# A hybrid attention and recurrence block on one core: attention in steps of one segment, and another split of the filler

## The chip, the cores and the metric

The kernel runs on one core of one Trainium2 chip. The core has five engines: PE (TensorE, matrix products), DVE (VectorE), ACT (ScalarE), POOL (GpSimd) and SP (SyncE, which here only issues DMAs). The time is the device time of one execution in microseconds, the lower the better; 4504.49 us is the median of 3 runs (4469.48 to 4522.03).

## What is computed

The input x is 4096 x 1024 in float32; 16 learned rows stand ahead of it, so T = 4112. After an RMS norm, one matrix product with w_in gives the inputs of two branches. The reference, cut to what matters:

```python
u = rmsnorm(h, norm_w)
p = u @ w_in                                  # 1024 columns to q, k, v, forget logits, gates, r, k, v, ...
# attention, 8 heads of 64, block of 128 queries, causal
s = q @ k.T / 8 + c[q] - c[k]                 # c: running sum of log sigmoid(forget logits)
o = softmax(where(k_pos <= q_pos, s, -1e30)) @ v * silu(z)
# recurrence, 8 heads, S is 64 x 64, one step per row
S = S * w_t + (S @ a_t) b_t + v_t k_t;  y = S @ r_t        # then group norm, bonus, silu gate
out = rmsnorm(h + concat(o, y) @ w_out, final_norm_w)[16:]
```

## The kernel before, in words

The kernel is one program; the order of instructions on every engine is made when it is built, by a planner that walks all instructions by priority (`tc.high_priority(offset=...)`, offsets in PR, L37: the larger the offset, the earlier) and places each when its inputs are ready in a model of the time. The `Ordered` wrapper (L54) around VectorE, ScalarE and TensorE adds ordering by hand: in mode "note" it remembers the last instruction, in mode "behind" it ties each new one after the remembered one.

Stages. (1) Weights are scaled and split into two float16 parts, x is normalised, split and transposed (to L384). (2) The recurrence (`rwkv_chain`, L818) in 33 sub-blocks of up to 128 rows, each of 4 chunks of 32 rows, each chunk in 3 hops: 387 hops. Beside every hop run the preparation of later sub-blocks (`beside`, L911) and filler: the generator `projections` (L636) makes the matrix products with w_in in four passes over 17 blocks of 256 rows. Pass 0 is the recurrence's own input (`in_proj`, L410), pass 1 q, k, v, z of heads 4 and 5 (`qk_block` L463, `vz_block` L480), pass 2 those of heads 0 to 3, pass 3 those of heads 6, 7 and the recurrence's gate (`gate_block`, L533). One unit of filler is 48 matmuls of 256 columns; a full block of passes 1, 2, 3 has 2, 4, 4 units. A hop is credited with RATE = 0.33 units (L941). (3) Attention. `head_load` (L986) fetches K, V and the column term cb of one 1024-key chunk of a head, `fetch` (L1108) calls it ahead of need, `projected` (L981) runs filler until the rows that are needed have been projected.

`attention(h, i, ...)` (L1014) is a generator for one block of 128 queries, W = 16 + 128 (i + 1) keys, in segments of SEG = 1024 keys (one to five). First part: for all segments scores on PE into ps_q (two buffers), and DVE's L1051 adds cb, writes sp and keeps the running maximum mt; L1057 makes nm. Second part, for all segments: ACT exponentiates sp in place (L1065), copies it to the high float16 part hl (L1071), POOL (60%) or DVE subtracts for the low part (L1076), and SP transposes hl into ht by DMA (L1078). Third part: the output matmuls ps_o, two for each 128 keys (L1086 to L1093), then row scale and gate (L1096 to L1101). Buffers: NSP = 9 of sp, NHL = 6 of hl and of ht. `advance` (L1191) runs the first part of block i, then the third part of block i - 1, then the second part of block i.

Between blocks of the first seven heads the loop at L1205 takes filler from `late` (the rest of `projections`, then `rwkv_out`, L1146, which multiplies the recurrence's half with w_out: 32 blocks of 128 rows, 24 matmuls of 512 columns each, counted 0.5 each) in proportion to the work done; `projected` takes from it without counting. In the last head (L1247), `out_prep` (L1225) and `out_rows` (L1236) do the attention's half of the output product, the sum, the last norm and the store, at the lowest priority.

Matmuls recorded at L67 were made while a mode of `Ordered` was set (in the recurrence), those at L92 without.

Of the kernel before, what the change touches and what calls it, by code (L numbers as in the profile page):

```python
# [40 lines left out]
NHL, NSP = 6, 9  # L41
# [6 lines left out]
RATE = 0.33  # L48
LEAD = 6
PARTS = ((0, 0), (0, 1), (1, 0))  # L50
# [26 lines left out]
def hymba_kernel(ctx: ExitStack, tc, x, meta, norm_w, w_in, b_f, mu_shift, w0, w_up, a0, a_up,  # L77
# [884 lines left out]
    with ExitStack() as fs:  # L962
# [18 lines left out]
        def projected(p, t):  # L981

            while done[PASS_OF[p]] * NB < min(t, SEQ + 1):
                next(late)
# [26 lines left out]
        nseg = 0  # L1011
        qz = {}

        def attention(h, i, head, dst):  # L1014

            nonlocal nseg
            p, hp = divmod(h, 2)
            q0 = 64 * hp
            if i % 4 == 0:
                g = min(4, NT - i)  # L1020
                t0 = N_META + i * P
                projected(p, t0 + g * P)
                Q = at.tile([P, 2, 4 * P], F16, tag="Q", name="Q")
                for a in range(2):
                    DQ.dma_start(Q[64 * a:64 * a + 64, :, :g * P],
                                 qk_d[p][a:a + 2, q0:q0 + 64, t0:t0 + g * P].rearrange("v p t -> p v t"))
                Zt = at.tile([P, 4, HD], F32, tag="Z", name="Zt")
                DQ.dma_start(Zt[:, :g], zf_d[p][t0:t0 + g * P, q0:q0 + 64].rearrange("(s t) e -> t s e", t=P))
                qz[h] = (Q, Zt)
            Q, Zt = qz[h]  # L1030
            W = N_META + P * (i + 1)
            qs = slice((i % 4) * P, (i % 4) * P + P)
            sps = []
            mt = at.tile([P, 8], F32, tag="mt", name="mt", bufs=4)
            ni = 0
            for a0 in range(0, W, SEG):
                sp = at.tile([P, SEG], F32, tag="sp", name="sp", bufs=NSP)
                sps.append(sp)
                for a in range(a0, min(a0 + SEG, W), 1024):
                    b = min(a + 1024, W)  # L1040
                    c, o = chunk(a)
                    o = a - o
                    ps = ps_q.tile([P, 1024], F32, tag="q", name="ps_q")
                    for a2 in range(a, b, 512):
                        b2 = min(a2 + 512, b)
                        dg = max(a2, min(b2, W - P))
                        for v in range(2):
                            mm(ps[:, a2 - a:b2 - a], Q[:, v, qs], head[c][0][:, a2 - o:b2 - o], v == 0, v == 1 and dg == b2)
# [237 lines left out]
```

## Time and profile before

| | us |
|---|---|
| median of 3 runs | 4504.49 |
| lowest, highest | 4469.48, 4522.03 |
| the profiled execution | 4462.28 |
| its span, first to last instruction | 4460.4 |
| PE busy | 3912.1 (88%) |
| DVE, ACT, POOL busy | 2956.9, 2122.7, 2230.5 |

Everything that follows is read from the one profiled execution. A busy time is the time in which an engine has a matmul or another operation in work; the ends of matmuls are modelled, so a run of short matmuls counts a little more than it takes. "PEclk" or "clock" is the granted share of TensorE's full clock. "DMA" is the mean busy share of the core's 16 DMA engines, where packets of different queues that overlap on one engine count twice, so that it can be over 1. In a line of waits stand the waiting operation, what ended the wait, the total in us, the number of waits and the longest.

### The profile page before, as it was taken

The page shows a single profiled execution, that of the slowest core. Times are in us where ns is not written, and L with a number is a line of the kernel's source. Part 1 is how long each engine was busy: PE and PEld are TensorE (multiplying, and loading weights), DVE is VectorE, ACT ScalarE, POOL GpSimd, SP SyncE. Part 2 cuts the span into 40 slices and gives each one's busy share as a digit, 9 for nine tenths or more (in the row PEclk, how much of TensorE's full clock was granted, in tenths as well). Part 3 has the DMA queues.
Part 4 walks back from the last instruction along what each step waited for, and adds up shares of the span by engine and source line. Part 5 has one row for each costly group of instructions (what it writes and reads, how often), then busy time and mean ns, then how long its engine had stood idle before and what let it go on. Part 6 is the DMA issues. An engine that isn't in the chain of part 4 may idle for free. (4 is left out here: it accounts for less than half of the span.)

```text
span 4460.4 us, 106426 instructions
## 1 busy us (share of the span) xinstructions
PE 3912.1 (88%) x42336; PEld 3012.8 (68%) x42336; DVE 2956.9 (66%) x6217; ACT 2122.7 (48%) x4338; POOL 2230.5 (50%) x3289
## 2 busy tenths in 40 slices
PE   5689999999989899998878878888888878978888
PEld 4577777777767677777656655666666656666566
DVE  5346665666667666752878978677787758646774
ACT  5433333333333233321666757577676747524552
POOL 4137565667666665762445545444454435332340
PEclk8899999999876899899999989999999989989989
DMA  9963223323222344324999999999999999999995
GB/s 265 262 172 93 79 79 97 87 75 90 74 70 79 85 138 121 98 88 141 196 213 229 216 193 227 199 216 227 208 212 234 212 203 223 258 270 242 198 218 185
DMA packets 1702644, 755.37 MB, mean 169 GB/s; under 512 B 1444601, under 2 KB 1639601, under 8 KB 1692162
## 3 DMA queue, kind: packets, MB, share of 16 engines
q1 hardware_dynamic: 1489346, 502.84, 55.8%
q10 hardware_dynamic: 194624, 170.08, 15.3%
q0 software_dynamic: 18176, 75.66, 5.6%
q8 instruction: 332, 5.44, 0.5%
q14 instruction: 166, 1.36, 0.1%
HBM read 278.97 MB, written 158.50 MB: 98 GB/s over the span
## 5 line engine op out<-in xcount | busy, mean ns | idle before, releaser
L1076 POOL TENSOR_TENSOR hl<-sp,hl 128x1024 f16<-128x1024 f32 (+7 forms) x384 | 719.7, 1881 | 517.3 <-ACT hl L1071 440.7
L1065 ACT ACTIVATE sp<-sp,nm 128x1024 f32<-128x1024 f32 (+8 forms) x672 | 644.5, 962 | 223.5 <-DVE nm L1057 175.6
L1071 ACT ACTIVATE hl<-sp 128x1024 f16<-128x1024 f32 (+8 forms) x672 | 568.2, 872 | 366.1 <-DMA ht<-hl 239.4
L92 PE MATMUL ps_o<-Vt,ht 128*128 128x64 f16 (+3 forms) x8960 | 559.5, 211 | 180.6 <-DMA ht<-hl 177.8
L92 PE MATMUL ps_q<-K,Q 128*128 128x512 f16 (+4 forms) x2432 | 596.9, 366 | 119.4 <-DVE mt L1051 118.3
L758 POOL TENSOR_TENSOR tm<-X,Am 128x248 f32<-128x248 f32 (+30 forms) x1023 | 498.1, 487 | 376.6 <-DMA Am<-a_d 290.1
L92 PEld LDWEIGHTS <-ht 128*128 128x128 f16 (+1 forms) x8960 | 466.9, 100 | 315.0 <-DMA ht<-hl 204.9
L92 PEld LDWEIGHTS <-wu 128*128 128x128 f16 (+1 forms) x5476 | 513.1, 102 | 194.8 <-ACT wu L160 28.1
L760 POOL TENSOR_TENSOR X<-X,tm 128x248 f32<-128x248 f32 (+30 forms) x1023 | 517.7, 506 | 76.6
L67 PEld LDWEIGHTS <-wu 128*128 128x128 f16 (+1 forms) x4988 | 454.5, 101 | 114.3 <-issue 26.0
L1051 DVE CUSTOM_DVE_ANT_0 sp<-ps_q,cb,mt 128x1024 f32<-128x1024 f32 (+8 forms) x416 | 436.1, 1048 | 80.3 <-PE ps_q L92 40.8
L1076 DVE TENSOR_TENSOR hl<-sp,hl 128x1024 f16<-128x1024 f32 (+8 forms) x288 | 383.2, 1333 | 99.3 <-ACT hl L1071 98.1
L92 PEld LDWEIGHTS <-Q 128*128 128x128 f16 x2432 | 221.8, 100 | 294.8 <-issue 150.2
L67 PE MATMUL ps_in<-fu,wu 128*128 128x256 f16 x3108 | 416.0, 285 | 3.4 <-DVE car L67 3.4
L1051 DVE CUSTOM_DVE_ANT_0 sp<-ps_q,cb,scs 128x1024 f32<-128x1024 f32 (+7 forms) x256 | 297.6, 1164 | 71.2 <-POOL hl L1076 43.9
L92 PE MATMUL ps_qk<-fu,wu 128*128 128x256 f16 x1632 | 237.7, 280 | 24.0 <-DVE t1k L500 18.5
L92 PE MATMUL ps_vz<-wu,fu 128*128 128x256 f16 x1644 | 247.6, 284 | 1.0 <-ACT th L544 0.6
L92 PE MATMUL ps_p<-OH,yH 128*128 128x512 f32 x512 | 221.5, 433 | 29.0 <-DVE oxt L1144 27.5
L1070 POOL MEMSET hl<- 128x224 f16 x256 | 72.4, 287 | 336.8 <-DMA ht<-hl 318.4
L92 PE MATMUL ps_zr<-fu,wu 128*128 128x256 f16 x1536 | 224.8, 285 | 8.0 <-DVE nm L1057 6.3
L67 PE MATMUL psz<-UV,SC 32*64 32x64 f32 (+1 forms) x4128 | 222.4, 232 | 3.0 <-ACT UV L67 2.2
L92 PE MATMUL ps_p<-OH,yL 128*128 128x512 f32 x512 | 209.6, 411 | 0.0
(350 smaller groups left out, 6976.6 us busy)
## 6 DMA issues: line engine op xcount, KB each, us to landing
fu<-u_d POOLq DMA_DIRECT2D x32, 1024.0 KB, 6.8
fu<-u_d SPq DMA_DIRECT2D x30, 1024.0 KB
pr<-p_d SPq DMA_DIRECT2D x32, 832.0 KB
p_d<-prt SPq DMA_DIRECT2D x96, 256.0 KB
u_d<-u SPq DMA_DIRECT2D x16, 1024.0 KB
Am<-a_d SPq DMA_DIRECT2D x128, 128.0 KB
Q<-qk_d ACTq DMA_DIRECT2D x128, 128.0 KB
oxt<-in_x_dram ACTq DMA_DIRECT2D x32, 512.0 KB
```

The source lines that it names most:

```text
L67: r = f(*args, **kw)
L92: PE.matmul(o, lhsT=l, rhs=r, start=start, stop=stop)
L758: G.tensor_tensor(out=tm[:, :, :k], in0=bc(X[:, :, s:s + 1], [P, 8, k]), in1=bc(Am[:, s * C + s + 1:s * C + C].unsqueeze(1), [P, 8, k]), o ...
L760: G.tensor_tensor(out=X[:, :, s + 1:], in0=X[:, :, s + 1:], in1=tm[:, :, :k], op=ALU.add)
L1051: V.tensor_tensor_reduce(out=sp[:, a - a0:b - a0], in0=ps[:, :b - a], in1=head[c][2][:, a - o:b - o], scale=scs[:, p, 0, hp:hp + 1], scala ...
L1065: A.activation(sp[:, :n], sp[:, :n], AF.Exp, bias=nm[:, 0:1], accum_out=nm[:, 1 + a // SEG:2 + a // SEG])
L1070: G.memset(hl3[:, :, n:], 0.0)
L1071: A.activation(hl3[:, 0, :n], sp[:, :n], AF.Copy)
L1076: eng.tensor_tensor(out=hl3[:, 1, :n], in0=sp[:, :n], in1=hl3[:, 0, :n], op=ALU.subtract)
```

## The change

`attention`, `finish` and `advance` go. In their place `pipeline()` makes one step for each segment: the scores of segment sg of the next block (`scores`, PE in mode "note"), then the weights of segment sg of this block (`weights`: exponential, copy, subtract, transpose), then the output products of the segment that was put aside LAG = 6 steps earlier (`output`, whose first matmul is tied behind the last scores matmul made). The arithmetic of the three is as before. Buffers: hl 5 (was 6), sp 7 (was 9), ht 9 (was 6), nm 12 (was 8), Zt 3 (was 2), o1 2 (was 4). Q and Zt of the next four blocks are loaded two blocks ahead. Filler: RATE falls to 0.265, four units (AHEAD) are taken before the first step, a step takes its share at once rather than a block, `projected` counts what it takes, a block of `rwkv_out` counts 1.0. The last head's output rows follow the blocks whose outputs have been made. Cut to its core (`scores`, `weights` and `output` hold the statements of `attention` and are shortened):

```diff
-NHL, NSP = 6, 9
+NHL, NSP, NHT = 5, 7, 9
-RATE = 0.33
+AHEAD = 4
+RATE = 0.265
+LAG = 6
         def projected(p, t):
+            nonlocal spent
             while done[PASS_OF[p]] * NB < min(t, SEQ + 1):
-                next(late)
+                spent += next(late)
+        def load_q(n):
+            if n >= len(steps) or n in qz:
+                return
...
+            Zt = at.tile([P, 4, HD], F32, tag="Z", name="Zt", bufs=3)
...
+        def scores(n, sg):
...
+            if sg == 0:
+                fetch(hx, i)
+                load_q(n - n % 4)
+                if n % 4 == 2:
+                    load_q(n + 2)
...
+        def weights(n, sg):
...
+            ht = at.tile([P, 2 * SEG // P, P], F16, tag="ht", name="ht", bufs=NHT)[:, :2 * nt]
+            hl = at.tile([P, 2 * SEG], F16, tag="hl", name="hl", bufs=NHL)[:, :2 * nt * P]
...
+            SP.dma_start_transpose(out=ht, in_=hl)
+        def output(n, sg):
...
+            PE.mode = "behind"
+            for j in range(nt):
...
+                mm(pso, ht[:k, j], Vj[:k], jt == 0, False)
+                PE.mode = None
+                mm(pso[:, 0:HD], ht[:k, nt + j], Vj[:k, 0:HD], False, jt * P + k == W)
...
                 for _ in rwkv_out(op, OW):
-                    yield 0.5
+                    yield 1.0
-        left = sum(max(0, NFULL - done[i]) * n for i, n in ((1, 2), (2, 4), (3, 4))) + 0.5 * NT
+        left = sum(max(0, NFULL - done[i]) * n for i, n in ((1, 2), (2, 4), (3, 4))) + NT
+        pend = []
+        def pipeline():
+            for n in range(-1, len(steps)):
+                ka = segs(n) if n >= 0 else 0
+                kb = segs(n + 1) if n + 1 < len(steps) else 0
+                for sg in range(max(ka, kb)):
+                    if sg < kb:
+                        PE.mode = "note"
+                        scores(n + 1, sg)
+                        PE.mode = None
+                    if sg < ka:
+                        weights(n, sg)
+                        pend.append((n, sg))
+                    while len(pend) > LAG or pend and pend[0][0] < n - 4 or (n == len(steps) - 1 and sg == ka - 1 and pend):
+                        output(*pend.pop(0))
+                    if sg < ka:
+                        yield n, min(SEG, width_of(steps[n][1]) - sg * SEG) + 2 * P // ka
+        allwork = 7 * sum(width_of(i) + 2 * P for i in range(NT))
+        with tc.high_priority(offset=PR[5]):
+            while spent < AHEAD:
+                spent += next(late)
+        while now < 7 * NT:
+            with tc.high_priority(offset=PR[3]):
+                now, cols = next(att)
+            work += cols
+            with tc.high_priority(offset=PR[5]):
+                while spent * allwork < work * left:
...
+        while True:
+            with tc.high_priority(offset=PR[4]):
+                if next(att, None) is None:
+                    break
+            output_rows((pend[0][0] if pend else len(steps)) - 7 * NT)
+        output_rows(NT)
+        out_rows(NT - 1, *ready)
```

## Rows read from the trace of the kernel before

**Rows 1.** Stages: us; PE, PEld, DVE, ACT, POOL busy (count); clock, DMA share, GB/s

```profile
400.00:1983.00 1583.00, 1524.65 (x19788) 1197.39 (x19785) 1022.48 (x2241) 519.32 (x1299) 1033.36 (x2026) 0.91 0.32 89
1983.00:2083.00 100.00, 99.92 (x915) 89.20 (x914) 28.43 (x76) 17.05 (x42) 30.41 (x43) 1.00 0.30 111
...
2126.00:3610.00 1484.00, 1251.79 (x13128) 931.26 (x13125) 1160.41 (x2446) 1010.22 (x1949) 716.72 (x673) 0.93 1.14 215
...
3740.00:4061.00 321.00, 275.77 (x1826) 201.66 (x1825) 188.32 (x357) 140.30 (x248) 118.98 (x95) 0.92 1.17 262
4061.00:4361.00 300.00, 249.08 (x1882) 181.74 (x1881) 210.41 (x379) 163.68 (x289) 104.22 (x81) 0.91 1.05 214
4361.00:4460.00 99.00, 86.43 (x392) 68.20 (x390) 49.75 (x74) 24.62 (x44) 8.11 (x15) 0.97 0.50 184
```

**Rows 2.** PE in order of time, at the recurrence's end: start, us, what

```profile
1982.55 0.66 PE L67 MATMUL psd<-ident,Y 128*128 128x128 f32 x4
1983.28 5.41 PE L67 MATMUL ps_vz<-wu,fu 128*128 128x256 f16 x48
1988.53 5.40 PE L67 MATMUL ps_qk<-fu,wu 128*128 128x256 f16 x48
```

**Rows 3.** ACT in order of time, from there to the first softmax block

```profile
2083.41 1.18 ACT L891 ACTIVATE Yt<-psd,gbT,gwT 128x32 f32<-128x32 f32 x4
...
2084.62 8.52 ACTq L995 DMA_DIRECT2D K<-qk_d  x10
...
2123.92 0.41 ACT L1065 ACTIVATE sp<-sp,nm 128x144 f32<-128x144 f32 x1 [0.39 <-DVE nm L1057]
```

**Rows 4.** Output matmuls ps_o alone, by stretches of one head: us, PE, DVE, ACT busy

```profile
2350.00:2588.00 238.00, 70.22 (x1120) 6.83 (x32) 6.65 (x32) 0.94 1.15 218
...
3615.00:3940.00 325.00, 69.82 (x1072) 6.46 (x32) 6.46 (x32) 0.91 1.14 228
3940.00:4361.00 421.00, 80.53 (x1311) 7.01 (x34) 7.01 (x34) 0.92 1.08 232
```

**Rows 5.** DMA queues, 2126 to 3610 us (q1 SP, q10 ACT, q0 POOL): packets, MB, share

```profile
q1 hardware_dynamic: 857200, 215.47, 84.1%
q10 hardware_dynamic: 91392, 48.60, 16.4%
q0 software_dynamic: 12624, 53.23, 12.5%
```

**Rows 6.** Waits from 2126 to 3610 us: total, times, longest

```profile
ACT hl L1071 <- DMA ht<-hl: 173.2, 92, 15.9
...
PE ps_o L92 <- DMA ht<-hl: 113.8, 59, 11.0
...
PE ps_q L92 <- DVE mt L1051: 96.0, 85, 7.1
...
DVE sp L1051 <- POOL hl L1076: 45.5, 20, 15.7
```

**Rows 7.** Waits of SP's queue in the same stretch

```profile
SPq L1078 <- PE ps_o L92: 170.5, 84, 7.7
```

**Rows 8.** Matmuls ps_p alone after the attention

```profile
4361.00:4460.00 99.00, 79.75 (x336) 62.10 (x336) 19.05 (x29) 0.97 0.50 184
```

**Rows 9.** Filler matmuls by shape, PE, 2126 to 3610 us: busy, mean ns, idle before

```profile
L92 PE MATMUL ps_vz<-wu,fu 128*128 128x256 f16 x1443 | 221.0, 285 | 1.0 <-ACT th L544 0.6 <-DVE t1k L500 0.3
L92 PE MATMUL ps_qk<-fu,wu 128*128 128x256 f16 x1488 | 215.2, 278 | 5.2 <-DVE qk L475 2.7 <-DMA fu<-u_d 2.4
L92 PE MATMUL ps_zr<-fu,wu 128*128 128x256 f16 x1344 | 198.6, 287 | 7.4 <-DVE nm L1057 6.3 <-ACT th L544 1.2
```

**Rows 10.** One output row block in the chain that ended last

```profile
4375.16 5.73 PE ps_p L92 x24
```

**Rows 11.** ACT's DMA queue from 3740 to 4361 us

```profile
q10 hardware_dynamic: 71360, 85.46, 50.3%
```

**Rows 12.** The 200 us of a head with the largest DMA share

```profile
3200.00:3400.00 200.00, 173.01 (x1889) 131.18 (x1888) 151.53 (x315) 138.76 (x266) 96.23 (x87) 0.95 1.19 227
```

More of the change, by code (lines that the diff above doesn't have):

```diff
@@ L1105, in hymba_kernel @@
+        nseg, npe, spent = 0, 0, 0
+        steps = [(hx, i) for hx in range(8) for i in range(NT)]
+        rows = {}
+        width_of = lambda i: N_META + P * (i + 1)
+        segs = lambda n: -(-width_of(steps[n][1]) // SEG)
+        qz, yos = {}, {}
         heads = {h: {} for h in range(8)}
-        need = lambda i: chunk(N_META + P * (i + 1) - 1)[0]
+        need = lambda i: chunk(width_of(i) - 1)[0]
         def fetch(x, i):
@@ L1113, in fetch @@
                         heads[HEADS[xx]][c] = head_load(HEADS[xx], c)
+        def load_q(n):
+            if n >= len(steps) or n in qz:
+                return
+            hx, i = steps[n]
+            h = HEADS[hx]
+            p, hp = divmod(h, 2)
+            q0 = 64 * hp
+            t0 = N_META + i * P
+            projected(p, t0 + 4 * P)
+            Q = at.tile([P, 2, 4 * P], F16, tag="Q", name="Q")
+            for a in range(2):
+                DQ.dma_start(Q[64 * a:64 * a + 64], qk_d[p][a:a + 2, q0:q0 + 64, t0:t0 + 4 * P].rearrange("v p t -> p v t"))
+            Zt = at.tile([P, 4, HD], F32, tag="Z", name="Zt", bufs=3)
+            DQ.dma_start(Zt, zf_d[p][t0:t0 + 4 * P, q0:q0 + 64].rearrange("(s t) e -> t s e", t=P))
+            qz[n] = Q, Zt
@@ L1191, in advance @@
-        def advance(hx, i):
-            nonlocal before, yo
-            h = HEADS[hx]
-            fetch(hx, i)
-            if i % 4 == 0:
-                yo = at.tile([P, 4, HD], F32, tag="yo", name="yo")
-            gen = attention(h, i, heads[h], yo[:, i % 4])
-            next(gen)
-            finish()
-            next(gen)
-            before = h, i, gen, yo
-        yo = None
-        for hx in range(7):
-            for i in range(NT):
-                with tc.high_priority(offset=PR[3]):
-                    advance(hx, i)
-                work += i + 2
-                with tc.high_priority(offset=PR[5]):
-                    while spent * 7 * NT * (NT + 3) < work * 2 * total:
-                        cost = next(late, None)
-                        if cost is None:
-                            break
-                        spent += cost
+        pend = []
@@ new lines, in hymba_kernel @@
+        att = pipeline()
+        work, now = 0, -1
+        allwork = 7 * sum(width_of(i) + 2 * P for i in range(NT))
[8 more added lines that the diff above has]
+                while spent * allwork < work * left:
+                    cost = next(late, None)
+                    if cost is None:
+                        break
+                    spent += cost
```

210 lines of the change are left out of this document (93 added, 117 removed).

## The prediction

> **What bounds the kernel now.** I first cut the span by stage [rows 1]. From 400 to 1983 us runs the recurrence with the projections as filler: PE is busy 1524.65 of 1583 us, 96%. Then come 100 us in which PE is 99.92 us busy and nothing of the recurrence is left: matmuls ps_vz and ps_qk in runs of 48 [rows 2]. They are filler that was credited to the recurrence and found no room in it. The last normalisation waits behind them: its first ACT step (L891) starts at 2083.41, the first K load right behind it at 2084.62, the first exponential of the attention at 2123.92 [rows 3]. The reader is to see that the attention starts some 100 us after the recurrence has ended, and that PE isn't idle in that time.
>
> Then six heads take 2126 to 3610 us, 247 each (one stands in [rows 4]: 1120 output matmuls make a head), with PE busy 1251.79 of 1484, 84.4% [rows 1]. The DMA column reads 1.14 there, and the queues add up to it: SP's transposes 84.1% of the engines' span, ACT's loads 16.4%, POOL's 12.5% [rows 5]. So two resources are nearly full in a head. What keeps PE from the rest of its time stands in the waits [rows 6]: 113.8 us on a transposed tile ht, 96.0 on DVE's read-out of the scores (mt). Its roots lie further back: ACT waits 173.2 us for an hl buffer that a transpose still reads, and SP's queue waits 170.5 us on PE for an ht buffer [rows 7]. The six ht and six hl buffers go round with the transposes and catch each other.
>
> The end is the worst part. From 3740 to 4061 DMA reads 1.17, while the second half of the output projection (32 row blocks) pushes through beside the attention; head 6 takes 325 us and head 7 421 [rows 1, 4]. Then 14 row blocks (336 matmuls ps_p, 24 to a block) run alone in the last 99 us [rows 8].
>
> **The change part by part.** *Start (RATE, AHEAD).* The recurrence has 387 hops (32 sub-blocks of 12, one of 3). The credit falls from 0.33 to 0.265 of a unit per hop, from 127.7 to 102.6 units: 25.1 units leave. A unit is 48 matmuls; the runs of 48 start 5.24 us apart [rows 2], so 25.1 units are 132 us of PE. The 915 matmuls of the 100 us [rows 1] are 19 units: they go from there entirely. The other 6 units (32 us) leave gaps inside the recurrence; its end moves by 0 (the chain of hops sets it) to 32 us (PE sets it, busy 96%). I take 0, since a hop now gets less to do beside it and nothing else in it gets shorter. The last normalisation must still run and the first loads land, 42 us in the trace (2083 to 2126). The four units of AHEAD, 21 us, are put into that time: nothing if the order lets them fill it, 21 us if they stand ahead of the normalisation. First transposes then come at 1983 + 42 = 2025, or 1993 to 2046 at the ends: 100 us earlier.
>
> *Filler per head.* Passes 1 to 3 of the projections are 161 units (16 blocks of 2, 4 and 4, and the short ones). Of the 127.7 credited before, 67 went to pass 0's last ten blocks, 32 to pass 1, 28 to pass 2; some 89 (the 4275 matmuls of [rows 9] over 48) lie in the six heads, 14.8 in each. After, 102.6 - 67 = 35.6 are done by then and 125 are left; less the 4 of AHEAD, spread over seven heads, 17.3 in each. The output projection's 32 blocks count 1.0 instead of 0.5 and so come 4.6 to a head on the mean, in the last head and a half of the seven, where before half of them fell into head 7. The third head needs pass 2 complete at i = 18, 64 units; 4 + 2.34 x 22 - 3 = 52 are paced by then, so some 12 units (63 us of PE) come in one run ahead of its loads. They are now counted as spent, so later steps get less: I take 0 for it, 30 us if the transposes run dry meanwhile.
>
> *PE in a head.* Busy time without filler is (1251.8 - 89 x 5.24) / 6 = 130.9 us. With 17.3 x 5.24 = 90.7 and 4.57 blocks at 5.73 us for 24 matmuls [rows 10], 26.2, it is 247.8 us, at the granted clock of 0.93 that I keep. Idle time now is (1484 - 1251.8) / 6 = 38.7 us: 19.0 on ht, 16.0 on mt, 3.7 else. Six steps between weights and output in place of one block (a single step in rows i < 8, four in the long ones), and nine ht buffers in place of six, attack the 19.0. It is bounded by 0 and 19; I take a quarter, 4.8, because the longest transposes wait (11.0 us) is well under six steps of 247 / 84 = 2.9 us. The mt wait has no reason to fall: two score buffers as before. So 247.8 + 24.5 = 272 us.
>
> *DMA in a head.* Packet time now is 113.0% of 1484 / 6, 279.5 us. POOL's queue pays 185.5 us for 89 units, 2.08 each: 2.5 more units are 5.2. The output projection's blocks I price from 3740 to 4361, where ACT's queue has 50.3% of 621 us, 312 [rows 11]; less the heads' own loads (16.4% of 1484 is 243, 40.6 a head, for 1.2 heads 49), 264 us moved 32 blocks of 1.5 MB (yr, zr, x in, the sum out) and 18 final ones of 1.25 MB: 3.7 us a MB, 5.6 a block, 25.7 a head. Together 310 us; at the present 1.13 that is 275 us, at the 1.19 of the best 200 us [rows 12] 262. [...] I take 270 between the two, near PE's 272.
>
> *Buffers (hl 6 to 5, sp 9 to 7, ht 6 to 9).* ACT waits for hl 173.2 us already [rows 6]. With a transposes stream that stalls less the smaller ring costs nothing; without, see the rivals. *Order on PE.* The first output matmul of a step is tied behind the scores. If the scores stand for mt, the outputs behind them stand too, then all filler behind those; DVE's read-out is then late by the same time. It costs 0 while mt waits stay at 16 us a head, and what they grow by otherwise; I take 0. Scores, subtracts, exponentials and loads keep their number; Q loads come two blocks earlier on ACT's queue, at the same size.
>
> *Head 7 and the end.* DMA: transposes 84.1% of 247 = 208, loads 41, 32 final blocks x 1.25 MB x 3.7 = 148: 397 / 1.13 = 351 us. PE: 130.9 + 32 x (5.73 + 0.9 for transposing and splitting; the tail's blocks take 99 / 14 = 7.1, stalls included) = 343, plus 24.5 idle = 367. With some 11 us for the last block's loads and store, 378. Now head 6's rest and head 7 cost 850 us from 3610.
>
> Sum: 2025 + 7 x 270 + 378 = 4293, with the 1.9 us outside the span 4295, against 4462.28 of the profiled execution (span 4460.4): 0.9625 of it. The median of the runs shown is 4504.49, 0.95% above the profiled one, so I state 4335.
>
> **The rivals.** *The transposes are the bound and stay so.* Each queue keeps its share: 275 to 280 us a head, head 7 with 385, since final blocks and transposes slow each other: 2030 + 7 x 278 + 385 = 4361, in the median's terms 4402. For it speaks that SP's queue alone fills 84.1%; against it, its waits for buffers, 170.5 us. [...]
>
> *Idle time is carried, not removed.* The waits on ht become waits on mt, PE stays 84.4% busy: 247.8 / 0.844 = 293.6 a head, 2025 + 2055 + 385 = 4465: no change, the 132 us moved out of the recurrence come back. The change then doesn't do what its order is for. For it: mt already has 85 waits.
>
> *The shallower rings turn it around (slower).* Place: hl. A transpose that lands late holds one of five, not six, hl buffers; ACT's copy stands, DVE's subtract behind it, then the read-out that shares DVE's queue, then the scores, and behind them, tied, the outputs that were ready. Price: it decides from (4460 - 2025 - 385) / 7 = 293 us a head on, that is 45 us idle, 0.54 us for each of 84 steps, where now it is 0.46. At 0.75 us a step a head is 311 us: 2025 + 2177 + 390 = 4592, 4635 in the median's terms. For it: 173.2 us ACT for hl and 45.5 us DVE for sp [rows 6]. Against it: an ht buffer is now free earlier than it is asked for, and that shortens hl's stay. [...]
>
> **How the numbers follow.** Forecast 4335 with its own range 4220 to 4400: 0.58. Transposes bound, 4402: 0.18. Carried idle, about 4500: 0.11. Shallow rings, 4635: 0.13. Below: recurrence 32 us shorter, 262 us a head and 350 at the end give 1993 + 1834 + 350 = 4177, 4217 in the median's terms; I go a little lower, 4200. Above, 4510 takes in the carried idle and leaves out the shallow rings and little else. A measurement of this kernel can tell about 1% from no change. Faster by over 1%: 0.76; within 1%: 0.11; slower by over 1%: 0.13.
>
> **What would show it.** Right: no stretch of pure ps_qk and ps_vz runs after the recurrence, first transposes by 2050; ps_o waits on ht under 60 us over all heads, SP's waits on PE for ht nearly gone; heads at 260 to 280 us with all filler, rwkv blocks included, done before head 7; end part under 400 us. Wrong: the first transposes not before 2080; mt waits over 250 us; a DMA share at 1.14 or less with heads of 290; ACT's waits for hl well over those now.

## The result, and the profile after

The changed kernel takes 4521.60 us (median; 4486.44 to 4579.00) where the kernel before takes 4468.85 in the same series: ratio 1.0128, interval 1.0101 to 1.0155. Ratios here and below leave out executions in which the core was in a slower state, while medians count all. The kernel is slower by 1.3%; 4335 us had been forecast, with a range of 4200 to 4510. Its profiled execution took 4546.54 us, with a span of 4544.8. The forecast had the start of the attention and nearly the amount of work right; PE's idle time, which it expected to shrink, grew.

First the stages of the changed kernel (the columns as in [rows 1]; the seven lines in the middle are heads 0 to 6, then head 7 and the tail):

```profile
400.00:1983.00 1583.00, 1496.86 (x19575) 1173.01 (x19573) 1023.63 (x2235) 518.47 (x1293) 1022.20 (x2021) 0.91 0.31 87
1983.00:2003.00 20.00, 14.47 (x120) 12.12 (x121) 7.50 (x22) 3.59 (x9) 5.32 (x12) 0.83 0.62 161
...
2003.00:2258.00 255.00, 203.28 (x2018) 147.78 (x2016) 191.81 (x409) 160.61 (x312) 117.66 (x105) 0.90 1.04 207
2258.00:2513.00 255.00, 224.49 (x2344) 170.08 (x2343) 195.20 (x425) 165.80 (x321) 125.08 (x121) 0.95 1.11 218
2513.00:2852.00 339.00, 281.67 (x2896) 218.59 (x2895) 225.69 (x494) 181.92 (x352) 156.76 (x161) 0.93 0.89 187
2852.00:3113.00 261.00, 212.86 (x2183) 157.83 (x2184) 206.95 (x417) 170.63 (x325) 119.96 (x115) 0.89 1.10 210
3113.00:3365.00 252.00, 213.28 (x2251) 161.73 (x2250) 193.49 (x398) 170.09 (x334) 119.76 (x108) 0.93 1.10 216
3365.00:3780.00 415.00, 354.91 (x3388) 279.33 (x3387) 229.03 (x465) 206.04 (x416) 156.88 (x154) 0.95 0.84 175
3780.00:4150.00 370.00, 298.88 (x2150) 211.51 (x2151) 226.09 (x445) 171.90 (x312) 134.13 (x106) 0.88 1.14 242
...
2003.00:4150.00 2147.00, 1789.36 (x17225) 1346.85 (x17223) 1468.26 (x3050) 1226.99 (x2368) 930.22 (x869) 0.92 1.02 206
4150.00:4545.00 395.00, 337.54 (x2453) 247.72 (x2450) 291.38 (x522) 213.26 (x389) 130.77 (x116) 0.94 0.93 221
...
2003.00:4545.00 2542.00, 2126.91 (x19674) 1594.57 (x19671) 1759.64 (x3571) 1440.25 (x2756) 1061.00 (x985) 0.92 1.00 209
```

The same stage of the kernel before, from its first softmax block to the end:

```profile
2124.00:4460.00 2336.00, 1969.27 (x18396) 1463.60 (x18393) 1697.90 (x3470) 1414.91 (x2702) 1004.32 (x921) 0.93 1.10 219
```

The reader is to see three things. The 100 us of pure filler [rows 1, 2] are gone: the attention starts at 2003, 121 us earlier than before [rows 3]. From 400 to 1983 PE is now busy 1496.86 us where it was 1524.65 [rows 1], at the same clock (0.91) and in the same 1583 us: 28 us of work have left a stretch that got no shorter by it. And the attention pays for both. Its busy time grows from 1969 to 2127 us, by 158, for 1278 more matmuls; its idle time (stretch less busy) grows from 367 to 415 us, by 48. Together: -121 + 158 + 48 = +85 us, the whole difference of the two spans (4544.8 - 4460.4 = 84). These are two single executions: that of the changed kernel is 25 us over its median, that of the kernel before 7 under, so 31 of the 84 us lie in which execution was profiled, and 53 between the medians. Busy and idle times below carry deviations of that size.

The waits, by the same view as [rows 6, 7] but over the whole attention (2124 to 4460 us), before:

```profile
ACT hl L1071 <- DMA ht<-hl: 239.4, 117, 15.9
...
PE ps_o L92 <- DMA ht<-hl: 177.8, 87, 11.0
...
PE ps_q L92 <- DVE mt L1051: 118.3, 104, 7.1
...
DVE sp L1051 <- POOL hl L1076: 69.1, 32, 15.7
...
SPq L1078 <- PE ps_o L92: 225.7, 107, 7.7
```

and after (2003 to 4545 us):

```profile
ACT hl L1102 <- DMA ht<-hl: 188.8, 100, 9.7
PE ps_q L69 <- DVE mt L1078: 178.8, 118, 14.7
...
PE ps_o L69 <- DMA ht<-hl: 118.7, 56, 8.3
...
DVE sp L1078 <- POOL hl L1107: 38.6, 30, 4.3
...
SPq L1108 <- POOL hl L1107: 418.7, 122, 145.3
...
SPq L1108 <- PE ps_o L94: 187.3, 94, 11.5
```

The waits on ht fell by 59 us and the waits on mt rose by 60: 296.1 us (177.8 and 118.3) became 297.5. PE stands as long at the two operands together as before, only more of it at the other one.

So the 48 us of new idle time are not in these two waits. They are in many small ones. Idle time ahead of the projections' filler went from 19 to 47 us (matmuls ps_vz, ps_qk, ps_zr and the small ones of their weights, pss and psb); the rest stands ahead of the output projection's matmuls (ps_p) and ahead of scores and outputs, for other operands. Two groups of matmuls carry most of it (busy us, mean ns, then PE's idle us before it and what ended that), before:

```profile
L92 PE MATMUL ps_vz<-wu,fu 128*128 128x256 f16 x1554 | 234.8, 284 | 1.0 <-ACT th L544 0.6 <-DVE t1k L500 0.3
...
L92 PE MATMUL pss<-onesb,wu 128*128 128x1 bf16 x64 | 3.2, 166 | 2.3 <-ACT wu L160 2.3
```

and after:

```profile
L94 PE MATMUL ps_vz<-wu,fu 128*128 128x256 f16 x1968 | 280.9, 284 | 20.0 <-DVE qk L477 8.7 <-ACT th L546 7.8 <-DVE t1k L502 3.5
...
L69 PE MATMUL pss<-onesb,wu 128*128 128x1 bf16 x48 | 2.3, 166 | 14.7 <-ACT wu L162 14.7
```

The filler waits for its own read-outs and weights on DVE and ACT, engines that the attention uses at the same time. And two waits fell: ACT's for hl (188.8 us, from 239.4) and DVE's for sp (38.6, from 69.1), although both rings have become smaller.

One line stands out: SP waits 145.3 us once. In that stretch (first all work, then the scores alone: PE, DVE) the attention stands still:

```profile
3525.00:3670.00 145.00, 135.81 (x1337) 119.89 (x1336) 25.35 (x62) 31.79 (x84) 31.03 (x46) 0.99 0.32 107
...
3525.00:3670.00 145.00, 0.17 (x1) 0.00 (x0) 0.99 0.32 107
```

`out_weights` loads w_out's tiles `wt` (L1158) into buffers of the sp ring. Four of the seven are taken until the last projection has been made and OH (L1159) can be written; with three left, the attention can't go on. It looks like the culprit.

### The profile page after: what moved, and what is told of

The parts are those of the page before. It is cut to its first block, busy times and chain, and to the rows that moved or that the text cites. A ratio compares the mean times of both kernels' runs of the same rounds, so it can differ in the third digit from the quotient of the medians.

```text
span 4544.8 us, 106304 instructions
## 1 busy us (share of the span) xinstructions
PE 3937.3 (87%) x42336; PEld 3023.9 (67%) x42336; DVE 2983.7 (66%) x6217; ACT 2128.2 (47%) x4338; POOL 2237.3 (49%) x3289
## 5 line engine op out<-in xcount | busy, mean ns | idle before, releaser
L1107 POOL TENSOR_TENSOR hl<-sp,hl 128x1024 f16<-128x1024 f32 (+7 forms) x384 | 737.4, 1927 | 469.1 <-ACT hl L1102 369.9
L69 PE MATMUL ps_q<-K,Q 128*128 128x512 f16 (+4 forms) x2432 | 610.3, 372 | 187.7 <-DVE mt L1078 178.8
L1102 ACT ACTIVATE hl<-sp 128x1024 f16<-128x1024 f32 (+8 forms) x672 | 565.8, 870 | 312.8 <-DMA ht<-hl 188.8
L94 PE MATMUL ps_o<-Vt,ht 128*128 128x64 f16 (+2 forms) x8288 | 531.4, 212 | 0.0
L94 PEld LDWEIGHTS <-ht 128*128 128x128 f16 (+1 forms) x8288 | 440.8, 101 | 85.2 <-issue 22.0
L1078 DVE CUSTOM_DVE_ANT_0 sp<-ps_q,cb,scs 128x1024 f32<-128x1024 f32 (+7 forms) x256 | 297.4, 1163 | 51.7 <-PE ps_q L69 33.2
L94 PE MATMUL ps_vz<-wu,fu 128*128 128x256 f16 x2040 | 290.6, 284 | 20.0 <-DVE qk L477 8.7
L94 PE MATMUL ps_qk<-fu,wu 128*128 128x256 f16 x1992 | 277.8, 279 | 3.7 <-DVE qk L477 1.7
L69 PE MATMUL ps_o<-Vt,ht 128*128 128x128 f16 (+1 forms) x672 | 152.2, 228 | 127.9 <-DMA ht<-hl 118.7
L94 PEld LDWEIGHTS <-fu 128*128 128x128 f16 x2232 | 208.3, 102 | 61.9 <-issue 19.8
```

Source lines behind the costliest of these rows:

```text
L69: r = f(*args, **kw)
L94: PE.matmul(o, lhsT=l, rhs=r, start=start, stop=stop)
L1078: V.tensor_tensor_reduce(out=sp[:, :b - a], in0=ps[:, :b - a], in1=head[c][2][:, a - o:b - o], scale=scs[:, p, 0, hp:hp + 1], scalar=(-3e3 ...
L1102: A.activation(hl3[:, 0, :nn], sp[:, :nn], AF.Copy)
L1107: eng.tensor_tensor(out=hl3[:, 1, :nn], in0=sp[:, :nn], in1=hl3[:, 0, :nn], op=ALU.subtract)
```

## The experiments

Every kernel has its own time against the kernel before in the same series. "Old" is the order of the kernel before, "new" that of the change; rings, the numbers of buffers, are sp/hl/ht. Start, busy and idle are those of the profiled execution: the first softmax block's row scale, and PE's busy and idle time from there to the end; "ht" and "mt" are PE's waits of ps_o on ht and of ps_q on mt. One execution of each kernel was profiled; it lies up to 40 us from the median (e4_sp9 31 under, f3_sp9_rate 20 over, i2_sp7_pool 40 over), so single differences of some 30 us in these columns show little.

| kernel | order, rings, RATE | median us | ratio (interval) | start | busy | idle | ht | mt |
|---|---|---|---|---|---|---|---|---|
| before | old 9/6/6 .33 | 4469 | 1 | 2124 | 1969 | 367 | 178 | 118 |
| after | new 7/5/9 .265 | 4521.6 | 1.0128 (1.0101-1.0155) | 2003 | 2127 | 415 | 119 | 179 |
| e1_wt_own | after, wt apart | 4517.4 | 1.0106 (1.0036-1.0175) | 1997 | 2118 | 416 | 128 | 166 |
| e2_rate | new 7/5/9 .33 | 4503.7 | 1.0094 (1.0061-1.0127) | 2115 | 1973 | 399 | 140 | 167 |
| e3_before_rate | old 9/6/6 .265 | 4517.1 | 1.0109 (1.0044-1.0173) | 2018 | 2103 | 394 | 188 | 129 |
| e4_sp9 | new 9/5/7 .265 | 4463.0 | 0.9975 (0.9934-1.0017) | 1994 | 2095 | 342 | 105 | 145 |
| f1_level | after, filler's priority | 4638.5 | 1.0389 (1.0325-1.0452) | 1988 | 2161 | 486 | 116 | 253 |
| f2_sp9_level | e4, filler's priority | 4630.6 | 1.0375 (1.0300-1.0450) | 1989 | 2150 | 478 | 161 | 229 |
| f3_sp9_rate | new 9/5/7 .33 | 4475.1 | 1.0016 (0.9978-1.0054) | 2110 | 1969 | 414 | 193 | 138 |
| f4_no_tie | after, no tie | 4570.4 | 1.0228 (1.0164-1.0292) | 1995 | 2129 | 446 | 196 | 162 |
| g1_sp9_28 | new 9/5/7 .28 | 4445.1 | 0.9925 (0.9888-0.9962) | 2049 | 2041 | 357 | 143 | 131 |
| g2_before_sp7 | old 7/6/8 .33 | 4419.8 | 0.9878 (0.9842-0.9915) | 2128 | 1960 | 343 | 147 | 120 |
| g3_lag3 | e4, LAG 3 | 4515.4 | 1.0113 (1.0074-1.0151) | 1989 | 2110 | 400 | 196 | 100 |
| g4_oldrings | new 9/6/6 .265, LAG 5 | 4468.6 | 0.9997 (0.9964-1.0030) | 2003 | 2106 | 377 | 125 | 139 |
| h1_sp7_only | old 7/6/6 .33 | 4412.0 | 0.9873 (0.9835-0.9911) | 2131 | 1955 | 317 | 122 | 128 |
| h2_before_rings | old 7/5/9 .33 | 4483.5 | 1.0032 (1.0002-1.0063) | 2133 | 1951 | 398 | 200 | 124 |
| h3_best_28 | old 7/6/8 .28 | 4495.1 | 1.0068 (1.0037-1.0099) | 2046 | 2057 | 378 | 144 | 139 |
| h4_after_hl6 | new 7/6/8 .265 | 4523.9 | 1.0137 (1.0089-1.0185) | 1984 | 2117 | 404 | 129 | 181 |
| i1_pool | after, POOL 100% | 4582.9 | 1.0261 (1.0188-1.0334) | 1995 | 2134 | 446 | 138 | 197 |
| i2_sp7_pool | h1, POOL 100% | 4491.9 | 1.0046 (1.0005-1.0088) | 2126 | 1979 | 425 | 219 | 153 |

**The stop of 145 us.**

```diff
-                wt = at.tile([P, SEG], F32, tag="sp", name="wt", bufs=NSP)[:, :D]
+                wt = ow.tile([P, D], F32, tag="wt", name="wt", bufs=2)
```

> The changed kernel, with the four w_out rows (wt) loaded into two buffers of their own instead of four of the seven sp buffers. Theory A (between 3525 and 3674 us the attention stands because wt holds four sp buffers until the last projection has been made): no stretch without ps_q longer than 20 us, head 5 falls from 415 to under 300 us, total 4390 to 4440 against 4521 of the changed kernel. Rival B (the 29 units of filler that run in this stretch have to run anyway, and PE is the bound): the stretch fills with attention, but heads 6 and 7 grow by as much, total 4490 or more.

The stop goes, and nothing is won: 4517 against 4522 us. The whole attention of this run:

```profile
1997.00:4531.00 2534.00, 2117.89 (x19682) 1594.44 (x19679) 1766.08 (x3572) 1437.88 (x2759) 1052.54 (x985) 0.92 1.03 209
```

Idle is 416 us, and 415 without the edit. In the stop PE had been busy 135.81 of 145 us, with filler that must run in any case; without the stop it runs elsewhere in the attention. The longest wait in the trace was no loss.

**Which part costs: filler moved or order.** RATE back to 0.33 in the changed kernel, and RATE 0.265 in the kernel before.

```diff
-RATE = 0.265
+RATE = 0.33
```

> The changed kernel with RATE back at 0.33, all else as changed. Theory A expects the stretch without scores in head 5 to stay, shorter by the filler that is no longer behind (some 60 instead of 149 us), and head 2 without its run of filler: first transposes near 2105, total 4440 to 4480. Theory C (the order in steps is what costs, not the filler): heads as long as in the changed kernel and the start 100 us later, total 4560 or more.

> The kernel before with RATE 0.265 alone. If a head of the old order can take 22 units instead of 15 the 100 us of the start are a gain: 4370 to 4400. If a head takes no more than it has (some 16 units), the 25 units come back as runs of filler ahead of the loads of the third head and at the end: 4440 to 4500, within 1% of the kernel before.

The first is 1.0094 (4504), the second 1.0109 (4517): the order with its rings alone costs about 1%, the moved filler alone costs about 1%, and both together (1.0128) hardly more than either, so they act on each other. Both are outside what was expected: e2_rate lies between its two theories, e3_before_rate 17 us over the higher one. A credit also changes the sequence that the planner makes, and no run parts the moved filler from that. The second is the nearest view of the filler alone. Its attention:

```profile
2018.00:4515.00 2497.00, 2103.26 (x19605) 1580.61 (x19602) 1763.55 (x3561) 1432.26 (x2752) 1046.59 (x979) 0.93 1.03 211
```

It starts 106 us earlier, is busy 134 us more and idle 27 us more: +55. The idle share of the stretch is 15.8%, and was 15.7%. In this order filler did not fill idle time: it came with its own, as if every unit cost its busy time divided by 0.84.

**The rings, in the new order.**

```diff
-NHL, NSP, NHT = 5, 7, 9
+NHL, NSP, NHT = 5, 9, 7
```

> The changed kernel with nine sp and seven ht buffers instead of seven and nine (the same memory). Theory A: with wt in four of nine, five are left, as in the kernel before, and the attention goes on: the stretch of 149 us without scores shrinks to under 40, total 4410 to 4470. Rival B: total within 1% of the changed kernel's. If ht at seven matters, SP's waits on PE for ht rise well over the 173 us of the changed kernel.

4463 us: the loss goes (0.9975). Both waits fall, ht to 105.0 and mt to 144.9 us, and the attention reads

```profile
1994.00:4431.00 2437.00, 2094.81 (x19687) 1580.92 (x19684) 1764.66 (x3572) 1438.40 (x2759) 1045.71 (x985) 0.94 1.05 218
```

against 2126.91 busy and 415 idle for the same work in the changed kernel. With the old rings and five steps the new order gives 4469 (edit against e4_sp9):

```diff
-NHL, NSP, NHT = 5, 9, 7
-LAG = 6
+NHL, NSP, NHT = 6, 9, 6
+LAG = 5
```

> The new order with the rings of the kernel before: nine sp, six hl, six ht, and output products five steps back, so that six ht buffers do. If hl is a second place where the shorter ring costs (ACT waits 206 us for hl in e4_sp9): under e4_sp9 by 0.3 to 1%, 4420 to 4450 us. If ht is what counts in the new order, one ht buffer less costs: 4480 to 4510. If neither, within 0.3% of e4_sp9's 4463.

It is 0.1% over e4_sp9: the third of the cases, neither hl nor ht counts here. The ring of hl in the new order, with sp kept at seven:

```diff
-NHL, NSP, NHT = 5, 7, 9
+NHL, NSP, NHT = 6, 7, 8
```

> The changed kernel with six hl and eight ht (sp stays at seven). If hl is part of the loss (ACT waits 177 us for hl in the changed kernel): 0.5 to 1% under it, 4475 to 4500 us. If the ring of sp alone makes the loss, as e4_sp9 suggests: within 0.4% of the changed kernel, 4505 to 4540.

4524 us, nothing won. So in the new order the kernels with nine sp (4463, 4469) are faster than those with seven (4522, 4524). In none of these runs was sp changed alone: with the two sp buffers go two ht buffers the other way, and a ring of ht cut from nine to seven with sp kept was not tried. Of the 114 us between the profiled spans of the changed kernel and e4_sp9, 59 are in the medians.

**Room in the heads.** The filler's priority was raised to that of the attention, in the changed kernel and in e4_sp9.

```diff
-PR = (300000, 290000, 295000, 100000, 3000, 97000, 100000, 3000)
+PR = (300000, 290000, 295000, 100000, 3000, 100000, 100000, 3000)
```

> The changed kernel with its filler at the same priority as the attention's steps (100000 in place of 97000). In the changed kernel a head without a run of projections carries 14 to 18 units in about 250 to 260 us, not the 22 that it is paced with, and the rest comes back in runs ahead of the loads of the third head (339 us) and the sixth (415 us). Theory A (the planner's order leaves the filler out, and PE has the room): heads carry about 22 units in 265 to 280 us, no run in the third and the sixth head, all of the recurrence's output blocks done before the last head, 4380 to 4440 us, ratio to the kernel before of 0.98 to 0.995. Theory B (a head's room is real: buffers and transposes hold a head that carries 22 units to some 295 us, the 0.88 to 0.93 us that a step loses with every tie and wait): the runs go, but the heads grow by as much; 4490 to 4540 us, ratio 1.005 to 1.015. If filler stands ahead of scores and holds up the chain of scores, weights and transposes (theory C), a head is over 300 us and the time over 4560.

> The changed kernel with nine sp and seven ht buffers, as in e4_sp9 (4463 us), and the filler at the attention's priority. If the order is a second cause beside the ring of sp (theory A), this one goes well under the kernel before: heads of 265 to 275 us with 20 to 22 units each, the recurrence's output blocks spread over heads 6 and 7 and none left for the last, 4330 to 4400 us. If the room in a head is set by transposes and PE together (theory B), it stays at e4_sp9's time within 1%, 4430 to 4500 us.

Both are slower than the kernel before by almost 4%, and f2_sp9_level is far over both of its expectations; the theory that the order of the planner merely left room unused falls. The first two heads of f1_level:

```profile
1988.00:2349.00 361.00, 296.02 (x2846) 230.06 (x2844) 221.61 (x476) 176.53 (x346) 142.47 (x148) 0.93 0.88 176
2349.00:2690.00 341.00, 278.65 (x2873) 214.35 (x2871) 207.71 (x474) 180.67 (x348) 142.50 (x149) 0.91 0.92 179
```

In head 0, 828 more matmuls than in the changed kernel are 93 us more busy and 13 more idle (65 against 52); the waits on mt reach 253 us over the attention, and idle time 486. That is theory C of f1_level, filler ahead of the scores that holds up what follows them: head 0 takes 361 us and the whole 4638.5. The 0.88 to 0.93 us a step of its theory B were the author's estimate, and no row shows them: in the changed kernel's heads without a run (0, 1, 3 and 4) PE is idle 30.5 to 51.7 us, 0.36 to 0.62 us for each of the 84 steps.

**The tie and the distance.** Without the tie:

```diff
-            PE.mode = "behind"
+            PE.mode = None
```

> The changed kernel without the tie of the first output matmul of a step behind the scores last made. If the tie costs nothing (the prediction's term, and the theory that the ring and the moved filler are the cause): within 1% of the changed kernel, 4490 to 4550 us, with the waits of the scores on DVE's read-out (161 us from 2100 on) about the same. If ready outputs stand behind scores that wait for DVE, PE loses less: these waits still there, but PE's total of waits down by 50 us or more and the time under 4470. If the tie is what keeps order good, outputs drift ahead and the time is over 4570.

Slower by 1% more, just over the 4570 us of the third case; the tie is a gain. The ht waits are back (195.8 us), the mt waits barely lower (161.7). With three steps in place of six, on e4_sp9:

```diff
-LAG = 6
+LAG = 3
```

> e4_sp9 with output products three steps back in place of six. If the distance of six is what takes the ht waits away (prediction), three steps of some 2.9 us are 8.7 us, under the longest transposes' wait of 11 us: the waits of ps_o on ht grow from 102 to 150 us or more and the time by as much, 4500 to 4530 us. If waits only change their name (ht for mt), the time stays within 0.5% of e4_sp9: 4440 to 4485.

```profile
PE ps_q L69 <- DVE mt L1078: 100.4, 77, 6.3
...
PE ps_o L69 <- DMA ht<-hl: 195.8, 76, 8.6
```

This run shows the exchange most plainly: against e4_sp9's 144.9 and 105.0, mt falls by 45 us and ht rises by 91. The distance buys 46 us net in these two waits, and idle falls from 400 to 342. So both hand-made ties of the change are worth about 1%; what the change loses, it loses elsewhere.

**The credit, in the new order, and the 28 free us.** On e4_sp9, with 0.33 in the first run and, as shown, 0.28 in the second:

```diff
-RATE = 0.265
+RATE = 0.28
```

> The changed kernel with nine sp and seven ht buffers and the old credit of 0.33 in the recurrence: the new order of steps alone, on the old ring. Attention starts at some 2115 us. If the shorter ring was all that made the new order slower, and moving filler costs about 1% by itself (as e3_before_rate shows on the old order), this is 1 to 1.5% under e2_rate's 4504: 4430 to 4460 us, slightly faster than the kernel before. If the new order is itself worse than the old one, it stays at 4480 to 4510.

> The changed kernel with nine sp and seven ht buffers (as e4_sp9) and a credit of 0.28 in place of 0.265. From 400 to 1983 us PE is busy 1496.86 us in the changed kernel and 1524.65 before, over the same 1583 us: some 28 us of filler cost nothing there and now cost their own time in the attention. At 0.28 the recurrence is given 108.4 units in place of 102.6. Theory A (PE's time in the attention is a plain sum, so filler hidden in the recurrence is won whole): PE busy in 400 to 1983 back at some 1520, first softmax still before 2015, 25 to 30 us under e4_sp9: 4430 to 4445 us, ratio to the kernel before 0.990 to 0.995. Theory B (the heads set their own time, by transposes and buffers, whatever filler they carry): within 10 us of e4_sp9, 4455 to 4475.

On nine sp a credit of 0.33 gives 4475, 0.28 gives 4445 and 0.265 gives 4463. The middle one is the lowest of the new order (0.9925, 0.9888 to 0.9962; the interval touches that of e4_sp9, 0.9934 to 1.0017, so the gain over it is not sure). It came by another way than the first theory put it: PE is busy 1496.40 us from 400 to 1983, as at 0.265, but with 144 more matmuls than the changed kernel at a granted clock of 0.93 for 0.91, and the attention starts at 2049, not before 2015.

These two runs also limit what e3_before_rate seemed to say. From f3_sp9_rate to e4_sp9, the same move of filler (0.33 to 0.265) lets the attention start 116 us earlier and makes PE 126 us more busy, but its idle time falls, from 414 to 342 us:

```profile
2109.00:4494.00 2385.00, 1968.89 (x18445) 1466.07 (x18444) 1694.72 (x3468) 1421.31 (x2708) 1001.66 (x927) 0.92 1.09 214
```

By the rule of the old order it would have cost 126 / 0.84 - 116 = 34 us; the medians go from 4475 to 4463. So here filler that was moved did not bring idle time along. Nor is the exchange of ht for mt a fixed one: f3_sp9_rate has the new order and six steps, and waits 193.1 us on ht.

**The rings, in the old order.** Seven sp and eight ht in the kernel before, seven sp alone, and all of the change's rings:

```diff
-NHL, NSP = 6, 9
+NHL, NSP, NHT = 6, 7, 8
...
-                ht = at.tile([P, 2 * SEG // P, P], F16, tag="ht", name="ht", bufs=NHL)[:, :2 * nt]
+                ht = at.tile([P, 2 * SEG // P, P], F16, tag="ht", name="ht", bufs=NHT)[:, :2 * nt]
```

> The kernel before with the change's ring of seven sp buffers (hl stays at six, ht gets eight): the shorter ring on the old order alone. If the shorter ring by itself costs what e4_sp9 against the changed kernel shows (1.3 to 1.5%): 4510 to 4530 us, ratio 1.010 to 1.016, with more waits of DVE for sp on POOL's subtract (69 us now from 2126 on). If it only hurts in the new order, where the scores of the next block are made while this block's weights are: within 0.5% of the kernel before.

> The kernel before with seven sp buffers and nothing else changed (hl and ht six). If ht made g2_before_sp7 faster (1.2%), by taking waits of ps_o on ht (178 us before, 147 there): this one is no faster than the kernel before, 4465 to 4500 us, with ht waits at 170 us or more. If the shorter ring of sp itself is a gain in the old order, since scores can't run ahead of the outputs: near g2_before_sp7, 4415 to 4440.

> The kernel before with the change's rings: seven sp, five hl, nine ht. If deep ht is what counts: 4415 to 4440 us, as g2_before_sp7, and then the new order alone costs 1.5% or more (e2_rate has the same rings and credit: 4504). If five hl are a bottleneck: over g2_before_sp7 by 0.5 to 1.5%, 4440 to 4490, and the new order alone costs less.

Here the kernel with the shorter ring of sp is faster, against what I expected of g2_before_sp7: 4420 us with eight ht, 4412 with six, so the gain isn't from ht. In h1_sp7_only the waits on ht fall from 177.8 to 121.8 with mt near where it was:

```profile
PE ps_q L92 <- DVE mt L1051: 128.1, 98, 6.7
PE ps_o L92 <- DMA ht<-hl: 121.8, 76, 7.8
```

With hl at five and ht at nine the gain is gone (1.0032), and the waits on ht stand at 200 us:

```profile
PE ps_o L92 <- DMA ht<-hl: 200.2, 90, 21.7
PE ps_q L92 <- DVE mt L1051: 124.3, 100, 9.2
```

That is also the old order on the rings and the credit of e2_rate (1.0094), so on those rings the new order costs 0.6%.

Two sp buffers less are +1.2% in the new order (g4_oldrings to h4_after_hl6, the two going to ht, with five and six steps) and -1.3% in the old one. A ring's size is known to the planner, and such an edit moves the instructions of PE against each other: of the 42,336 matmuls in the traces of h1_sp7_only and of the kernel before, counted in order, 11,876 have other tiles at the same place, while the sequence of SP's DMAs is the same. What was measured as a ring is therefore the ring and another order of PE's instructions; these runs don't part the two.

**Do the gains add?** The rings of g2_before_sp7 with RATE 0.28:

> g2_before_sp7 with a credit of 0.28 (three changed constants against the kernel before). By the sum of PE's time nothing is won or lost when units leave the 100 us behind the recurrence for heads that are as full: of the 19.4 units that leave, 0 to 1 had cost nothing, so 4410 to 4440 us, level with g2_before_sp7 within 0.5%. If the heads have idle time that the units can fill, up to 19 units of 5.24 us are won, and 4330 to 4390 would show it.

No: 4495 us, 1.7% over g2_before_sp7, outside both expectations. It starts 82 us earlier, is busy 97 us more and idle 35 us more.

```profile
2046.00:4481.00 2435.00, 2057.18 (x19197) 1541.81 (x19194) 1725.31 (x3529) 1426.55 (x2733) 1028.93 (x959) 0.93 1.05 214
```

Idle was 343 of 2303 us (14.9%) and is 378 of 2435 (15.5%): in the old order, filler that is moved in comes with its own idle time once more.

**By what chain the scores wait.** One place of the changed kernel's trace, in order of time:

```profile
2337.72 1.06 ACT L1102 ACTIVATE hl<-sp 128x1024 f16<-128x1024 f32 x1 [6.67 <-DMA ht<-hl]
...
2338.81 1.22 DVE L1107 TENSOR_TENSOR hl<-sp,hl 128x1024 f16<-128x1024 f32 x1 [4.20 <-ACT hl L1102]
...
2340.18 1.34 DVE L1078 CUSTOM_DVE_ANT_0 sp<-ps_q,cb,mt 128x1024 f32<-128x1024 f32 x1
...
2341.58 0.95 PE L69 MATMUL ps_q<-K,Q 128*128 128x512 f16 x2 [0.28 <-DVE mt L1078]
```

A late hl buffer holds ACT's copy, the copy holds DVE's subtract, the subtract the read-out, and the read-out PE. At this place PE lost only 0.28 us by it, as filler filled the time; whether the long waits on mt come by the same chain was not followed. To cut it, all subtracts of full segments went to POOL:

```diff
-POOL_SHARE = 60
+POOL_SHARE = 100
```

> The changed kernel with all subtracts of full segments on POOL (60% before). If DVE's queue, standing at a subtract for ACT's copy, is what makes the scores wait: waits of ps_q on mt fall from 179 to 120 us or less, and the time by 0.7 to 1.5%, 4455 to 4490 us. If the read-out is late for another reason (sp buffers, the transposes' pace): mt waits stay over 150 us, and POOL's longer subtract (2.1 us against 1.3 for a full segment) makes it slower, 4520 to 4580.

```profile
PE ps_q L69 <- DVE mt L1078: 197.3, 108, 16.8
...
DVE sp L1078 <- POOL hl L1107: 140.3, 99, 18.0
```

The mt waits rise to 197 us, against the theory. The run doesn't settle it, since POOL takes 2.11 us for a subtract (at 2342.47 us of the changed kernel's trace) that takes DVE 1.22: what replaces the subtract on DVE's queue is a wait for the sp buffer that POOL's subtract still reads, 140.3 us where it was 38.6. On the fastest kernel:

> h1_sp7_only (the kernel before with seven sp buffers, 4412 us) with all subtracts of full segments on POOL. If DVE's queue is the chain in the old order too: mt waits from 128 to under 100 us, 4380 to 4405 us. If not, POOL's longer subtract holds hl buffers and sp buffers longer: 4415 to 4470.

4492 us, over both expectations; the same harm, with DVE's waits for sp at 113.4 us. The fastest of all runs stays h1_sp7_only, the kernel before with seven sp buffers: 4412 us, 1.3% under before and 2.4% under the changed kernel (4412.0 / 4521.6).

## Why the prediction was wrong, by its own steps

The sums that follow are those of the profiled execution, as the prediction's were.

**Start: right.** 2025 us had been taken, 1993 to 2046 as bounds; it is 2003. The recurrence's end didn't move, as taken.

**The 25 units: worked out rightly.** They were also priced where they arrive, as 17.3 units a head in place of 14.8. The 6 units from inside the recurrence are 28 us of work that had been free and became work in the attention. The 19 units of the 100 us stretch were no gain by themselves: PE was 99.92 of 100 us busy there. Work that has to be done is won only if it is put where PE would be idle. So the whole forecast gain hung on the next term but one, a fall of PE's idle time.

**PE busy in the heads: nearly right.** 7 x 247.8 = 1735 us were forecast, 1789 measured, 3% more. The granted clock in the heads was 0.92, not the 0.93 that was kept; by an estimate from these numbers that lets busy time grow as the clock falls (1789 x 0.01 / 0.93), that is some 19 of the 54 us.

**PE idle in a head: this step failed.** The prediction put it at 24.5 us, from 38.7 (4.8 on ht in place of 19.0, 16.0 on mt, 3.7 else), and then took 270 us a head, which leaves 155 us over seven heads. Measured: 2147 - 1789 = 358 us, 51 a head. PE's two main waits in the seven heads (2003 to 4150 us):

```profile
PE ps_q L69 <- DVE mt L1078: 166.8, 103, 14.7
PE ps_o L69 <- DMA ht<-hl: 101.0, 47, 8.3
```

That is 14.4 us a head on ht, 23.8 on mt, and 12.9 for all else. Each of the three terms missed by 8 to 10 us: ht fell by less than was taken, mt rose, and the small waits, kept at 3.7 without a reason while the heads got more filler, more than tripled. Together this is 203 us of the miss; with 54 of busy, 17 at the end (395 for 378) and 22 won at the start it makes the whole: 203 + 54 + 17 - 22 = 252 = 4545 - 4293. In the end part, 0.9 us a block for transposing and splitting and 11 us for the last block's loads and store were the author's estimates; the trace of before shows 0.62 to 0.76 us of PE for a block's four transposes (ps_t, L1233: 8.1 us for 52 after 4361, 14.5 for 76 from 3940 to 4361) and 7.9 us from the last matmul to the end of the span. "The mt wait has no reason to fall" was true, and the case that it rises was left to a rival. Over the whole attention it rose by 60 us, as much as ht fell (59). The tie and the distance are each worth about 1% (f4_no_tie, g3_lag3), but what ht gave back stands at mt; that the same rings feed both waits and so carry it over is argued, not shown.

The prediction's own signs part in the same way. Those of its right case on work and start came: no stretch of pure filler right behind the recurrence, the first transposes before 2050, the 32 output blocks of the recurrence done before head 7, an end part of 395 us. Those on waits did not: ps_o waits 119 us on ht, not under 60, and SP's waits on PE for an ht buffer went from 226 to 187 us, not to nearly nothing.

**DMA: no bound.** (310 / 1.19 is 261 us, not 262; nothing hangs on it.) The ordinary heads of 252 to 261 us have a DMA share of 1.04 to 1.11, under the 1.14 of before [rows 1] and far under the 1.19 of [rows 12]. The rival by which the transposes stay the bound, at 275 to 280 us a head, falls: the DMA engines were less full than before, and what a head waited for was not their total.

**The third head's run, costed 0: right as a loss, wrong in its size.** It was to be 12 units of 63 us. The head took 339 us, some 80 over its neighbours, with 57 us more busy than the fullest of them (281.67 against 224.49). Its idle share (57 of 339, 17%) lies among theirs (12 to 20%), so the run was work and no stall, work that other heads would have had to carry; for the sixth head and its stop e1_wt_own shows that.

**Buffers, costed 0: wrong.** "With a transposes stream that stalls less the smaller ring costs nothing." Nine sp and seven ht in place of seven and nine take off 1.3% (e4_sp9 against the changed kernel), and that alone would have made the change neutral. The place named for it by a rival, hl, was not it: h4_after_hl6 gives nothing, and ACT's waits for hl are shorter than before (188.8 us for 239.4). Its other side could not have been read from the trace of before: in the old order the shorter ring is a gain.

**The rival that came nearest** is "idle time is carried, not removed. The waits on ht become waits on mt, PE stays 84.4% busy": 1 - 415/2542 is 83.7%, and its 4500 us are 0.5% under the measured 4522. It had a chance of 0.11. Its nearness is in part luck: its own sum is 4465 us and the profiled execution took 4546.54, and it foretold no change, which is what e4_sp9 gives (0.9975); the rest of the loss goes with the rings, which were another rival's. What spoke for it stood in [rows 6]: two waits of about the same size on one engine.

**What stays open.** Why nine sp suit the new order and seven the old one. A kernel with another ring and the same sequence on PE was not tried: the planner makes the sequence from the rings. Nor was any run made of the smaller parts of the change (four units ahead, filler counted in `projected`, blocks of `rwkv_out` counted 1.0, the last head's rows, Q loaded earlier), and why the filler's own small waits grew was not followed.

## What to carry to other kernels

Work that fills a stretch is no idle time: before a filler is moved, ask how much of it was free where it is (28 us here) and what share of the target stage PE is really busy; price it at its busy time divided by that share at first (it fitted the old order, 0.84, and was too dear in the new one with nine sp). An edit that removes one of two main waits on one engine should be priced with the other wait taking over, until a run shows that the sum falls. And where a planner sets the order, a buffer count is an edit of the order too: measure it in both orders before giving it a sign.

## What the runs showed of the hardware

In the attention, idle time of PE and a low granted clock go together. Among the heads of the changed kernel, one with 30.5 us of idle time in 255 has a mean clock of 0.95, one with 51.7 in 255 has 0.90, and head 6, with 71 in 370, has 0.88; in the stop, where PE was fed with filler for 145 us, it was 0.99. The changed kernel and e4_sp9 run the same matmuls in the attention (x19674 and x19687 in their lines above). Where PE is idle 415 us, the granted clock is 0.92 and the work takes 2126.91 us; where it is idle 342, the clock is 0.94 and the same work takes 2094.81. So 73 us of idle time less came with 32 us of busy time less.

That the idle time is the cause is not shown by this pair. The two profiled executions lie on opposite sides of their medians, and one and the same kernel, the changed one, ran at 0.910 in one execution (4546.54 us) and at 0.920 in another (4486.44 us). Nor does the busy share by itself tell the clock: in the recurrence of the kernel before, PE is 93% busy for 200 us at 0.76:

```profile
1200.00:1400.00 200.00, 186.10 (x2450) 148.41 (x2449) 136.87 (x299) 68.61 (x164) 134.63 (x260) 0.76 0.27 75
```
